# A hybrid DeltaNet and attention block in fp32: VectorE's long elementwise steps made in pieces of at most 256 columns

## The chip, the cores and the metric

The kernel runs on one core of a Trainium2 chip. The metric is the device time of one execution in microseconds (us), lower is better. A core has engines that work side by side: TensorE (PE) for matrix products, with PEld its weight loads; VectorE (DVE), ScalarE (ACT) and GpSimd (POOL) for elementwise work; SyncE (SP), which issues the transfers. They wait for each other by semaphores. Each engine works through its own list of instructions in order.

## The reference

One layer with two groups of heads that read the same normalised input (512 latent tokens and 256 context tokens, 2048 wide) through one projection. Group A, where the change lies, has eight heads of gated DeltaNet: a short convolution over five tokens, silu, gates, and a chunked scan in both directions, added and normalised.

```python
def centred_conv(x, w):                      # five taps, one weight per channel
    pad = CONV_K // 2
    L = x.shape[1]
    xp = jnp.pad(x, ((0, 0), (pad, pad), (0, 0)))
    out = xp[:, 0:L] * w[0]
    for j in range(1, CONV_K):
        out = out + xp[:, j:j + L] * w[j]
    return out
...
    diff = g_c[..., :, None] - g_c[..., None, :]
    decay = jnp.where(incl, jnp.exp(jnp.where(incl, diff, 0.0)), 0.0)
    a = jnp.where(strict, jnp.einsum('nbhid,nbhjd->nbhij', k_beta, k_c) * decay, 0.0)
    t_inv = lax.linalg.triangular_solve(eye + a, ..., lower=True)
...
    def step(s, inp):
        v_new = u_i - jnp.einsum('bhcd,bhde->bhce', w_i, s)
        o_i = (... q_i * exp(g_i) @ s + intra_i @ v_new)
        s = (s * exp(g_last) + (k_i * exp(g_last - g_i))^T @ v_new)
        return s, o_i
...
    o_gdn = (o_lf + flip(o_lb)).astype(h.dtype)
    gdn_lat = (rms_norm(o_gdn, gdn_norm_w).reshape(B, L, GDN_WIDTH) * jax.nn.silu(z_g))
```

Group B is grouped-query attention with eight query heads; both go through one output projection, a gated residual and a last norm.

## The kernel before

**Stages.** Up to about 165 us the norms, the modulation and the first projection; 165 to 290 the first head's convolutions, the gates and its preparation; 290 to 805 the DeltaNet heads, each some 85 us; 805 to 940 the last scan and the preparation of attention; to 1240 attention; to 1412 the output projection.

**Products in three parts.** A fp32 weight piece of 128 x 512 is split into a high part (whi, cast on ScalarE, L122) and a low part (wlo, the difference, L123, made on VectorE for the first 14 pieces and on GpSimd after them); each product is three matmuls. A projection makes the columns of one head, for example k: kl is the latent half (512 columns, L157), kx the context half (256, L159), in 16 steps out of four weight pieces, so wlo_k1_3 is the last low piece for the k of the second head (heads count from 0).

**Convolution** (`conv`, L178). ScalarE copies the projection into craw (L184 the context, L187 the latent part) and makes the first tap for all columns (L195, cacc). VectorE adds taps 1 to 4, in place in cacc (L199): four steps over the 512 latent columns, and for k and v four more over the 256 of the context. ScalarE takes the tanh (L202, L203), VectorE finishes the silu (L212), which gives kq (k and q side by side), kc (k of the context) or vv.

**Preparation of a head** (`gdn_prep`). GpSimd subtracts the gate sums (L550), VectorE takes the minimum with two masks (L553), each over 6 chunks of 64 columns, ScalarE the exponential (L555); VectorE multiplies by a column for each row (L571, 768 columns) and by the products of k and q; then 32 x 32 transposes NT (L587), a series of small steps on NE (L607 to L609) and products for a triangular inverse, with transfers through DRAM in between (nd, NE, DD), ending in DTh (L632), pxah (L640) and UU. The first head's transposes t1h (L509) turn kq; tvh turns vv.

**Scan** (`gdn_scan`). Twelve steps a head. TensorE makes ksh from the state sth, VectorE the right side rh (L731), TensorE tsh (L740), ScalarE vsh (L744), TensorE tsh again (L751), VectorE the next state sth (L757; L755 for the first step). After the last step GpSimd and VectorE (L768) add the two directions, ScalarE takes four sums of squares (L770) and VectorE, GpSimd and ScalarE scale by the norm (L771, L209, L774).

**Order.** TensorE's order is written out: the scan of one head runs between projection matmuls for the next ones, so many columns of them at each yield. The other engines' instructions are put in order by a scheduler that works through what is ready by priority; scan steps on VectorE and ScalarE have high priority (`first_of_all`), the NE series a lower one, and the rest stands in program order of priority. In the attention stage all engines' order is written out. Buffers: cacc and craw rotate, ScalarE's and VectorE's conv steps thus wait for earlier readers.

Of the kernel before, what the change touches and what calls it, by code (L numbers as in the profile page):

```python
# [11 lines left out]
ALU = mybir.AluOpType  # L12
# [10 lines left out]
SEQ = 512  # L23
CTX = 256
# [44 lines left out]
def build(tc, a):  # L69
    nc = tc.nc  # L70
    V, S, G, T, SY = nc.vector, nc.scalar, nc.gpsimd, nc.tensor, nc.sync
# [27 lines left out]
    masks = (cmain[:, 256:320], cmain[:, 320:384])  # L99
# [78 lines left out]
    def conv(t, nm, pl, pc):  # L178

        n = SEQ + (CTX + 2 if pc is not None else 0)  # L180
        off = n - SEQ
        raw = next_craw()
        if pc is not None:
            S.copy(raw[:, 2:2 + CTX], pc)  # L184
        else:
            raw = raw[:, CTX + 2:]
        S.copy(raw[:, off + 2:off + 2 + SEQ], pl)  # L187
        acc = cvp.tile([128, 770], F32, tag="cacc", bufs=CA_BUFS, name=f"cacc_{nm}")
        acc = acc[:, :n]

        def w(j):
            return cvT[:, j * 24 + t:j * 24 + t + 1]

        e = raw[:, 2:]
        S.activation(acc, raw[:, 0:n], AF.Copy, scale=w(0))  # L195
        for i0, m in ((off, SEQ), (0, CTX))[:1 if pc is None else 2]:
            for j in range(1, 5):
                x = acc[:, i0:i0 + m]
                V.scalar_tensor_tensor(out=x, in0=raw[:, i0 + j:i0 + j + m], scalar=w(j), in1=x,  # L199
                                       op0=ALU.mult, op1=ALU.add)  # L200
        if pc is not None:
            S.activation(e[:, :CTX], acc[:, :CTX], AF.Tanh)  # L202
        S.activation(e[:, off:off + SEQ], acc[:, off:], AF.Tanh)  # L203
        return acc, e, off
# [9 lines left out]
    def mul(eng, out, x, y):  # L214
        eng.tensor_tensor(out=out, in0=x, in1=y, op=ALU.mult)  # L215
# [274 lines left out]
    def gdn_prep(h):  # L490
# [6 lines left out]
        gr = gp.tile([128, 12, 64], F32, tag="gr", bufs=1, name=f"gr{nm}")  # L497
# [27 lines left out]
        for p in range(2):  # L525
# [16 lines left out]
        cc = gp.tile([128, 3, 12], F32, tag="cc", bufs=2, name=f"cc{nm}")  # L542
        V.tensor_tensor(out=cc[:, 0].rearrange("p (v q) -> p v q", v=2),
                        in0=gsc["beta"][:, col].rearrange("p (v q) -> p v q", v=2),
                        in1=rk2.unsqueeze(1).to_broadcast([128, 2, 6]), op=ALU.mult)
# [3 lines left out]

        G.tensor_tensor(out=gr, in0=gr, in1=gsc["gcum"][:, col].unsqueeze(2).to_broadcast([128, 12, 64]),  # L550
                        op=ALU.subtract)
        for v in range(2):
            V.tensor_tensor(out=gr[:, v * 6:v * 6 + 6], in0=gr[:, v * 6:v * 6 + 6],  # L553
                            in1=masks[v].unsqueeze(1).to_broadcast([128, 6, 64]), op=ALU.min)
        S.activation(gr, gr, AF.Exp)  # L555

        yield
# [10 lines left out]
            for v in range(2):  # L568
                mul(V, IBv[pr, v, :, 64 - 64 * s:128 - 64 * s], gq[pr, :, 1], grv[pr, v, 2:6])
        AT = gr  # L570
        V.tensor_tensor(out=gr, in0=gr, in1=cc[:, 1].unsqueeze(2).to_broadcast([128, 12, 64]), op=ALU.mult)  # L571
        for v in range(2):
            mul(V, grv[:, v, 2:6], gq[:, :, 0], grv[:, v, 2:6])
        yield
# [28 lines left out]
        with tc.high_priority(offset=1500):  # L603
            for m in range(14, 0, -1):
# [3 lines left out]
                                in1=NE[:, m:m + 1, m + 1:].to_broadcast([96, m, n]), op=ALU.mult)  # L608
# [65 lines left out]
        for p in range(6):  # L674
            for half in range(2):
                b = half * 64
                for v in range(2):
                    i0, o0 = (b + 32, b) if v == half else (b, b + 32)
# [3 lines left out]
        for v in range(2):  # L682
            for half in range(2):
                b = half * 64
                i0, o0 = (b + 32, b) if v == half else (b, b + 32)
# [3 lines left out]
    def gdn_scan(h):  # L689
# [3 lines left out]
        ktok, vtok, cc, sq = pres[h]  # L693
        UU, IB = UUs[h % 2], IBs[h % 2]
        st = None
        o = None
        oq = gp2.tile([128, 2, 4, 128], F32, tag="oq", bufs=1, name=f"oq{nm}")
        osb = oq[:, 0]
        kss = stile([128, 2, 256], f"ks{nm}", "k")
        steps = [(0, 0), (0, 1), (1, 1), (1, 0)] + [(0, p) for p in range(2, 6)] + [(1, p) for p in range(5, 1, -1)]  # L700
        for si, (v, p) in enumerate(steps):
# [6 lines left out]
            if lat and o is None:  # L708
                o = stile([128, 4, 128], f"o{nm}", "o")
            if si == 0:  # L710
                r = vtok[:, p]
            else:
# [11 lines left out]
                with first_of_all():  # L724
# [5 lines left out]
                    for rows, d in halves:  # L730
                        V.scalar_tensor_tensor(out=r[rows], in0=ks[rows, d], scalar=gsc["negeg"][rows, gcol:gcol + 1],  # L731
                                               in1=vtok[rows, p], op0=ALU.mult, op1=ALU.add)
# [32 lines left out]
        oc = gp2.tile([128, 8, 64], F32, tag="oc", bufs=1, name=f"oc{nm}")  # L765
        jk = oc[:, 0:2].rearrange("p c t -> p (c t)")
        G.tensor_tensor(out=oq[:, 1], in0=osb, in1=oq[:, 1], op=ALU.add)
        V.tensor_tensor(out=osb, in0=oq[:, 1], in1=o, op=ALU.add)  # L768
        for p in range(4):
            S.activation(jk, osb[:, p], AF.Square, accum_out=ms[:, p:p + 1])  # L770
        V.scalar_tensor_tensor(out=ms, in0=ms, scalar=1.0 / 128.0, in1=sq, op0=ALU.mult, op1=ALU.add)  # L771
# [641 lines left out]
```

## Time and profile before

| | |
|---|---|
| median of 3 runs | 1405.37 us (1404.99 to 1408.5) |
| the profiled execution | 1413.92 us, its span 1412.1 us |
| TensorE matmuls, weight loads | 1282.5 and 1031.0 us busy, 9406 each |
| VectorE | 747.5 us busy, 1643 instructions |
| ScalarE | 608.3 us busy, 1509 instructions |
| GpSimd | 529.4 us busy, 477 instructions |
| mean granted clock of TensorE | 0.975 |

The page gives busy time by engine and slice; the trace answers which instruction ran when, how long, and what an engine waited for. A row of a timeline is one instruction, or several alike that follow each other; the bracket at its end tells how long the engine had been idle before, and who released it. PE stands for TensorE's matmuls. An instruction's duration includes work that overlaps the next one on its engine, so two starts in a row can be closer than the first one's duration.

### The profile page before, as it was taken

To read this page: it belongs to the slowest core of one execution; us is meant where nothing else is said; L and a number is where in the kernel's file an instruction comes from. 1 tells how busy PE (TensorE), PEld (TensorE's weight loads), DVE (VectorE), ACT (ScalarE), POOL (GpSimd) and SP (SyncE) were. 2 spreads that over 40 slices of the span, in tenths; PEclk is the share of its full clock that TensorE was granted. 3 is DMA by queue.
4 is the path that set the end of the run, shared out by engine and by line. 5 is a ranking of instruction groups with operands and counts; after the bars stand their busy time and mean duration, and the time that the engine had idled before them with its cause. 6 is when DMAs were issued, how large, how long until landed. Compare 5 with 4: busy or idle time off the path is not lost.

```text
span 1412.1 us, 24988 instructions
## 1 busy us (share of the span) xinstructions
PE 1282.5 (91%) x9406; PEld 1031.0 (73%) x9406; DVE 747.5 (53%) x1643; ACT 608.3 (43%) x1509; POOL 529.4 (37%) x477
## 2 busy tenths in 40 slices
PE   3788988999999999999999999889889999999997
PEld 1455676877788787787777877667777778787785
DVE  3434685475456656476665524427566655544322
ACT  4111342445444453544545444446556663433221
POOL 1011211334353453443434445435777772012330
PEclk9999998999999999999999999999999999999999
DMA  9999622222322223232232343353545432474202
GB/s 311 255 270 285 180 72 56 71 56 63 67 71 69 66 65 77 58 84 57 81 66 58 84 127 111 93 186 105 145 132 151 134 97 61 164 234 146 90 33 102
DMA packets 264187, 163.52 MB, mean 116 GB/s; under 512 B 63042, under 2 KB 236187, under 8 KB 263043
## 3 DMA queue, kind: packets, MB, share of 16 engines
q1 hardware_dynamic: 264067, 161.93, 41.6%
q8 instruction: 74, 1.21, 0.4%
q14 instruction: 46, 0.38, 0.1%
HBM read 148.33 MB, written 13.56 MB: 115 GB/s over the span
## 4 chain that ended last, share of the span: by engine, by line
PE 55%; DVE 17%; DMA 8%; issue 8%; ACT 7%; POOL 4%; SPq 2%; POOLq 0%; ACTq 0%; DVEq 0%
PE zl L1197 6%; PE vl L157 5%; DMA wada<-in_w_ada 4%; PE kl L157 3%; PE vx L159 3%; DVE cacc_k L199 2%; DVE cacc_v L199 2%; PE kvl L157 2%; PE po L140 2%; PE tsh L751 2%; PE po L141 2%; PE po L139 2%; PE ql L157 2%; PE kx L159 2%; PE tsh L740 2%
## 5 line engine op out<-in xcount | busy, mean ns | idle before, releaser
L215 POOL TENSOR_TENSOR sdh<-sth,egl 128x256 f32<-128x256 f32 x80 | 55.4, 692 | 169.5 <-DVE sth L757 75.8
L1238 POOL TENSOR_TENSOR gacc<-graw,gacc 128x512 f32<-128x512 f32 x60 | 89.3, 1488 | 43.3 <-ACT graw L1236 30.0
L736 ACT ACTIVATE oqh<-ksh,egsw 64x128 f32<-64x128 f32 x128 | 46.3, 362 | 99.0 <-DVE rh L731 98.2
L731 DVE SCALAR_TENSOR_TENSOR rh<-ksh,negeg,vtokh 64x128 f32<-64x128 f32 x176 | 61.1, 347 | 50.8 <-PE ksh L719 47.5
L1197 PE MATMUL zl<-hhL,whi_z 128*128 128x512 f32 x208 | 88.0, 423 | 0.0
L123 POOL TENSOR_TENSOR wlo_z<-wraw_z,whi_z 128x512 fp32r<-128x512 f32 x52 | 70.5, 1358 | 45.0 <-ACT whi_z L122 43.8
L1197 PE MATMUL zl<-hlL,whi_z 128*128 128x512 f32 x208 | 84.9, 408 | 0.0
L1197 PE MATMUL zl<-hhL,wlo_z 128*128 128x512 f32 x208 | 84.8, 408 | 0.1
L140 PE MATMUL po<-wlo_wo,mh 128*128 128x512 f32 x192 | 77.5, 404 | 3.7 <-DVE wlo_wo L123 3.7
L757 DVE TENSOR_TENSOR sth<-sdh,tsh 128x256 f32<-128x256 f32 x80 | 33.7, 421 | 87.1 <-PE tsh L751 81.7
L139 PE MATMUL po<-whi_wo,mh 128*128 128x512 f32 x192 | 76.0, 398 | 1.5 <-ACT whi_wo L122 1.5
L141 PE MATMUL po<-whi_wo,ml 128*128 128x512 f32 x192 | 76.8, 400 | 0.0
L123 DVE TENSOR_TENSOR wlo_wo<-wraw_wo,whi_wo 128x512 fp32r<-128x512 f32 x48 | 37.7, 794 | 66.5 <-ACT whi_wo L122 66.4
L816 DVE TENSOR_TENSOR ptl<-pt,pth 128x512 fp32r<-128x512 f32 x48 | 31.7, 687 | 72.5 <-ACT pth L815 72.4
L1344 POOL TENSOR_TENSOR yx<-yx,tt 128x512 f32<-128x512 f32 x12 | 17.1, 1443 | 126.9 <-DVE tt L215 67.6
L199 DVE SCALAR_TENSOR_TENSOR cacc_v<-craw,cvT,cacc_v 128x512 f32<-128x512 f32 (+1 forms) x64 | 44.0, 734 | 38.8 <-ACT cacc_v L195 38.5
L751 PE MATMUL tsh<-vsh,ktok 128*128 128x128 f32 x352 | 55.6, 281 | 3.6 <-ACT vsh L744 3.2
L323 POOL TENSOR_TENSOR wlo<-wraw,whi 128x384 fp32r<-128x384 f32 x16 | 16.0, 1006 | 110.4 <-ACT whi L322 110.4
L122 ACT CAST whi_wo<-wraw_wo 128x512 fp32r<-128x512 f32 x48 | 29.3, 618 | 61.4 <-PE po L141 37.7
L751 PEld LDWEIGHTS tsh<-vsh,ktok 128*128 128x128 f32 x352 | 47.8, 192 | 10.1 <-ACT vsh L744 4.6
L255 PE MATMUL ada<-wada,cs 128*32 128x256 f32 x512 | 42.3, 417 | 13.9 <-DMA wada<-in_w_ada 13.8
L744 ACT ACTIVATE vsh<-tsh,cch 128x128 f32<-128x128 f32 x88 | 32.2, 366 | 45.9 <-PE tsh L740 44.9
(488 smaller groups left out, 4162.2 us busy)
## 6 DMA issues: line engine op xcount, KB each, us to landing
wada<-in_w_ada SPq DMA_DIRECT2D x128, 256.0 KB, 5.1
graw<-in_w_ada SPq DMA_DIRECT2D x64, 256.0 KB, 2.7
wraw_z<-in_w_in SPq DMA_DIRECT2D x52, 256.0 KB, 3.1
wraw_wo<-in_w_out SPq DMA_DIRECT2D x48, 256.0 KB, 3.1
wraw_q<-in_w_in SPq DMA_DIRECT2D x28, 256.0 KB, 3.2
wraw_k<-in_w_in SPq DMA_DIRECT2D x28, 256.0 KB, 2.8
wraw_v<-in_w_in SPq DMA_DIRECT2D x28, 256.0 KB, 2.8
xs<-in_x SPq DMA_DIRECT2D x4, 1024.0 KB
```

What stands on the lines that cost most here:

```text
L123: (lo_eng or G).tensor_tensor(out=lo, in0=raw, in1=hi, op=ALU.subtract)
L139: T.matmul(out, lhsT=lh, rhs=rh, start=start, stop=False, skip_group_check=True)
L140: T.matmul(out, lhsT=lh, rhs=rl, start=False, stop=False, skip_group_check=True)
L141: T.matmul(out, lhsT=ll, rhs=rh, start=False, stop=stop, skip_group_check=True)
L157: T.matmul(pl, lhsT=lw, rhs=rt[0][:, k], start=st, stop=sp, skip_group_check=True)
L159: T.matmul(pc, lhsT=lw, rhs=rt[1][:, k], start=st, stop=sp, skip_group_check=True)
L199: V.scalar_tensor_tensor(out=x, in0=raw[:, i0 + j:i0 + j + m], scalar=w(j), in1=x, op0=ALU.mult, op1=ALU.add)
L215: eng.tensor_tensor(out=out, in0=x, in1=y, op=ALU.mult)
L731: V.scalar_tensor_tensor(out=r[rows], in0=ks[rows, d], scalar=gsc["negeg"][rows, gcol:gcol + 1], in1=vtok[rows, p], op0=ALU.mult, op1=ALU.add)
L751: T.matmul(ts[:, d], lhsT=ktok[:, p, half], rhs=vs, start=True, stop=True, skip_group_check=True)
L1197: T.matmul(pl, lhsT=lw, rhs=rt[:, k], start=st, stop=sp, skip_group_check=True)
L1238: G.tensor_tensor(out=acc, in0=raw, in1=acc, op=ALU.add)
```

## The change

Four places of VectorE work on fewer columns at a time, each with more instructions for the same result. In the conv the four latent steps are done for each half of the 512 columns (8 instructions in place of 4). The masks go over 3 chunks of 64 at a time (four of 192 columns in place of two of 384). The product over 768 columns goes in four of 192. The sum of the outputs goes in two of 256. In all VectorE has 1789 instructions in its list in place of 1645 (of which the profile records 1643): 128 are taken away and 272 added. TensorE's order stays the same in every instruction; the scheduler sets the others' order anew.

```diff
@@ conv
-        for i0, m in ((off, SEQ), (0, CTX))[:1 if pc is None else 2]:
+        for i0, m in ((off, 256), (off + 256, 256), (0, CTX))[:2 if pc is None else 3]:
             for j in range(1, 5):
                 x = acc[:, i0:i0 + m]
                 V.scalar_tensor_tensor(out=x, in0=raw[:, i0 + j:i0 + j + m], scalar=w(j), in1=x,
@@ gdn_prep
-        for v in range(2):
-            V.tensor_tensor(out=gr[:, v * 6:v * 6 + 6], in0=gr[:, v * 6:v * 6 + 6],
-                            in1=masks[v].unsqueeze(1).to_broadcast([128, 6, 64]), op=ALU.min)
+        for w0 in range(0, 12, 3):
+            V.tensor_tensor(out=gr[:, w0:w0 + 3], in0=gr[:, w0:w0 + 3],
+                            in1=masks[w0 // 6].unsqueeze(1).to_broadcast([128, 3, 64]), op=ALU.min)
         S.activation(gr, gr, AF.Exp)
@@ gdn_prep
-        V.tensor_tensor(out=gr, in0=gr, in1=cc[:, 1].unsqueeze(2).to_broadcast([128, 12, 64]), op=ALU.mult)
+        for w0 in range(0, 12, 3):
+            mul(V, gr[:, w0:w0 + 3], gr[:, w0:w0 + 3], cc[:, 1, w0:w0 + 3].unsqueeze(2).to_broadcast([128, 3, 64]))
@@ gdn_scan
-        V.tensor_tensor(out=osb, in0=oq[:, 1], in1=o, op=ALU.add)
+        for p in range(0, 4, 2):
+            V.tensor_tensor(out=osb[:, p:p + 2], in0=oq[:, 1, p:p + 2], in1=o[:, p:p + 2], op=ALU.add)
         for p in range(4):
             S.activation(jk, osb[:, p], AF.Square, accum_out=ms[:, p:p + 1])
```

Lines behind line 571 move by one, those behind 768 by two.

VectorE, where the k of head 5 is convolved while the scan of head 3 makes its steps 7 and 8 (heads and steps count from 0). Before:

```order
L199 SCALAR_TENSOR_TENSOR cacc_k5_5856<-craw0_1460,cvT_80,cacc_k5_5856 128x512
L757 TENSOR_TENSOR sth3_7_5927<-sdh3_7_5894,tsh3_7_5913 128x256
L199 SCALAR_TENSOR_TENSOR cacc_k5_5856<-craw0_1460,cvT_80,cacc_k5_5856 128x256
L212 SCALAR_TENSOR_TENSOR kq5_5852<-craw0_1460,cacc_k5_5856 128x4x64 x2
L212 SCALAR_TENSOR_TENSOR kc5_5853<-craw0_1460,cacc_k5_5856 128x2x64
L632 STREAM_TRANSPOSE DTh4_5744<-DDh4_5743 128x384
L731 SCALAR_TENSOR_TENSOR rh3_8_5942<-ksh3_5404,negeg_87,vtokh3_4646 64x128 x2
L212 SCALAR_TENSOR_TENSOR kc5_5853<-craw0_1460,cacc_k5_5856 128x2x64
```

And after the change, in the same place:

```order
L199 SCALAR_TENSOR_TENSOR cacc_k5_5944<-craw0_1460,cvT_80,cacc_k5_5944 128x256 x8
L758 TENSOR_TENSOR sth3_7_6019<-sdh3_7_5986,tsh3_7_6005 128x256
L199 SCALAR_TENSOR_TENSOR cacc_k5_5944<-craw0_1460,cvT_80,cacc_k5_5944 128x256
L212 SCALAR_TENSOR_TENSOR kq5_5940<-craw0_1460,cacc_k5_5944 128x4x64
L199 SCALAR_TENSOR_TENSOR cacc_k5_5944<-craw0_1460,cvT_80,cacc_k5_5944 128x256
L212 SCALAR_TENSOR_TENSOR kq5_5940<-craw0_1460,cacc_k5_5944 128x4x64
L732 SCALAR_TENSOR_TENSOR rh3_8_6034<-ksh3_5487,negeg_87,vtokh3_4716 64x128 x2
L633 STREAM_TRANSPOSE DTh4_5832<-DDh4_5831 128x384
L212 SCALAR_TENSOR_TENSOR kc5_5941<-craw0_1460,cacc_k5_5944 128x2x64 x2
```

The scan's rh of step 8 moved ahead of the transpose DTh and of both kc.

ScalarE, at the end of the scan of head 3 and the start of that of head 4, where the v of head 5 is convolved (whi_q1a is a weight piece for attention). Before:

```order
L770 ACTIVATE och3_6317,msh3_6316<-oqh3_5403 128x128 x3
L555 ACTIVATE grh5_6390<-grh5_6390 128x768
L770 ACTIVATE och3_6317,msh3_6316<-oqh3_5403 128x128
L774 ACTIVATE oqh3_5403<-oqh3_5403,msh3_6316 128x128 x4
L187 COPY craw0_1460<-vl5_6009 128x512
L744 ACTIVATE vsh4_0_6383<-tsh4_0_6381,cch4_5512 128x128
L184 COPY craw0_1460<-vx5_6010 128x256
L122 CAST whi_q1a_2_6455<-wraw_q1a_2_6453 128x512
L195 ACTIVATE cacc_v5_6355<-craw0_1460,cvT_80 128x770
```

And after the change:

```order
L772 ACTIVATE och3_6413,msh3_6412<-oqh3_5486 128x128 x4
L555 ACTIVATE grh5_6491<-grh5_6491 128x768
L776 ACTIVATE oqh3_5486<-oqh3_5486,msh3_6412 128x128 x4
L122 CAST whi_q1a_2_6556<-wraw_q1a_2_6554 128x512
L184 COPY craw0_1460<-vx5_6106 128x256
L187 COPY craw0_1460<-vl5_6105 128x512
L745 ACTIVATE vsh4_0_6484<-tsh4_0_6482,cch4_5595 128x128
L195 ACTIVATE cacc_v5_6452<-craw0_1460,cvT_80 128x770
```

All four squares now precede the exponential, and the weight cast and both copies precede vsh.

VectorE, in the first head's preparation (IB, grh and NTh are its tiles, q1 belongs to the second head). Before:

```order
L553 TENSOR_TENSOR grh0_1677<-grh0_1677,cmain_77 128x384 x2
L199 SCALAR_TENSOR_TENSOR cacc_q1_1697<-craw0_1460,cvT_80,cacc_q1_1697 128x512
L532 TENSOR_SCALAR skh0_1762<-ssh0_1680 128x2
L123 TENSOR_TENSOR wlo_k1_3_1908<-wraw_k1_3_1905,whi_k1_3_1907 128x512
L199 SCALAR_TENSOR_TENSOR cacc_q1_1697<-craw0_1460,cvT_80,cacc_q1_1697 128x512
L539 RECIPROCAL rk2h0_1769<-skh0_1762 128x6
```

And after the change, where wlo_k1_3 stands now:

```order
L212 SCALAR_TENSOR_TENSOR kq1_1707<-craw0_1460,cacc_q1_1709 128x4x64 x2
L215 TENSOR_TENSOR IB0_1575<-gqh0_1811,grh0_1689 64x4x64 x2
L215 TENSOR_TENSOR grh0_1689<-grh0_1689,cch0_1789 128x192 x4
L215 TENSOR_TENSOR grh0_1689<-gqh0_1811,grh0_1689 128x256 x2
L215 TENSOR_TENSOR grh0_1689<-gch0_1866,grh0_1689 128x128 x2
L588 STREAM_TRANSPOSE NTh0_1693<-grh0_1689 32x6x32 x4
L123 TENSOR_TENSOR wlo_k1_3_1929<-wraw_k1_3_1926,whi_k1_3_1928 128x512
```

The low weight piece moved from among the q1 conv steps to behind the transposes NTh.

## Rows read from the trace of the kernel before

**Rows 1.** The page, part 1: busy us, share of the span and instructions of each engine.

```profile
PE 1282.5 (91%) x9406; PEld 1031.0 (73%) x9406; DVE 747.5 (53%) x1643; ACT 608.3 (43%) x1509; POOL 529.4 (37%) x477
```

**Rows 2.** The windows by stage, of all engines. Columns: stretch, its length, then busy us and instructions of each engine, the granted clock of TensorE, the share of the DMA engines, GB/s.

```profile
165.00:290.00 125.00, 112.30 (x904) 93.27 (x903) 84.36 (x261) 51.82 (x147) 24.36 (x23) 0.93 0.27 64
...
550.00:635.00 85.00, 80.25 (x744) 66.93 (x743) 52.47 (x128) 40.58 (x114) 35.38 (x34) 1.00 0.28 69
```

**Rows 3.** TensorE's waits between 290 and 940 us: line that waited, whom it waited for, us in total, times, longest.

```profile
PE tsh L740 <- DVE rh L731: 14.3, 16, 2.1
PE ksh L722 <- DVE sth L755: 5.1, 4, 2.3
...
PE kvx L159 <- ACT craw L184: 3.0, 2, 2.6
```

**Rows 4.** The same in the first head's stretch, 165 to 290 us.

```profile
PE gtr L431 <- ACT egl L427: 2.5, 1, 2.5
PE pxah L640 <- DVE DTh L632: 2.2, 1, 2.2
PE gcp L416 <- issue: 1.9, 1, 1.9
```

**Rows 5.** VectorE's groups by line and form: busy us, mean ns of one, idle time before them.

```profile
L199 DVE SCALAR_TENSOR_TENSOR cacc_v<-craw,cvT,cacc_v 128x512 f32<-128x512 f32 x32 | 26.2, 819 | 38.6 <-ACT cacc_v L195 38.5
...
L199 DVE SCALAR_TENSOR_TENSOR cacc_q<-craw,cvT,cacc_q 128x512 f32<-128x512 f32 x32 | 24.1, 752 | 12.7 <-ACT cacc_q L195 12.4
L199 DVE SCALAR_TENSOR_TENSOR cacc_v<-craw,cvT,cacc_v 128x256 f32<-128x256 f32 x32 | 20.7, 648 | 0.2
L199 DVE SCALAR_TENSOR_TENSOR cacc_k<-craw,cvT,cacc_k 128x256 f32<-128x256 f32 x32 | 20.2, 632 | 0.1
```

**Rows 6.** Timeline of VectorE in the first head, the k conv between steps of the gates. Columns: start, duration in us, engine, line, instruction, count.

```profile
170.79 0.48 DVE L199 SCALAR_TENSOR_TENSOR cacc_k<-craw,cvT,cacc_k 128x256 f32<-128x256 f32 x1
171.19 0.22 DVE L400 RECIPROCAL s_g<-s_g 128x12 f32<-128x12 f32 x1
...
172.48 0.75 DVE L199 SCALAR_TENSOR_TENSOR cacc_k<-craw,cvT,cacc_k 128x512 f32<-128x512 f32 x1
173.14 0.17 DVE L403 TENSOR_SCALAR ug<-w_g 128x12 f32<-128x12 f32 x1
```

**Rows 7.** Timeline of VectorE, the q conv of a middle head, and one v conv of the second head.

```profile
237.88 4.33 DVE L199 SCALAR_TENSOR_TENSOR cacc_v<-craw,cvT,cacc_v 128x512 f32<-128x512 f32 x8 [2.00 <-ACT cacc_v L195]
...
573.38 2.33 DVE L199 SCALAR_TENSOR_TENSOR cacc_q<-craw,cvT,cacc_q 128x512 f32<-128x512 f32 x3 [2.96 <-ACT cacc_q L195]
575.74 0.42 DVE L757 TENSOR_TENSOR sth<-sdh,tsh 128x256 f32<-128x256 f32 x1
```

**Rows 8.** Timeline of TensorE, a middle head, where it waits for rh of step 8.

```profile
565.48 0.46 PE L740 MATMUL tsh<-rh,UU 128*128 128x128 f32 x2 [1.40 <-DVE rh L731]
```

**Rows 9.** Timeline of VectorE ahead of that.

```profile
561.77 2.27 DVE L212 SCALAR_TENSOR_TENSOR kq<-craw,cacc_k 128x256 f32<-128x256 f32 x2
563.97 0.28 DVE L212 SCALAR_TENSOR_TENSOR kc<-craw,cacc_k 128x128 f32<-128x128 f32 x1
564.17 0.57 DVE L632 STREAM_TRANSPOSE DTh<-DDh 128x384 f32<-128x384 f32 x1
564.67 0.67 DVE L731 SCALAR_TENSOR_TENSOR rh<-ksh,negeg,vtokh 64x128 f32<-64x128 f32 x2
```

**Rows 10.** Timeline of ScalarE at the change of scans in a middle head.

```profile
592.65 0.85 ACT L555 ACTIVATE grh<-grh 128x768 f32<-128x768 f32 x1 [0.81 <-POOL wlo_q1a L123]
593.40 0.29 ACT L770 ACTIVATE och<-oqh 128x128 f32<-128x128 f32 x1
...
595.11 1.28 ACT L774 ACTIVATE oqh<-oqh,msh 128x128 f32<-128x128 f32 x4 [1.32 <-POOL msh L209]
...
596.76 0.36 ACT L744 ACTIVATE vsh<-tsh,cch 128x128 f32<-128x128 f32 x1
...
597.79 0.95 ACT L195 ACTIVATE cacc_v<-craw,cvT 128x770 f32<-128x770 f32 x1
```

**Rows 11.** Timeline of TensorE there.

```profile
597.17 0.71 PE L751 MATMUL tsh<-vsh,ktok 128*128 128x128 f32 x4 [0.81 <-ACT vsh L744]
...
600.21 0.70 PE L722 MATMUL ksh<-sth,kc 128*128 128x256 f32 x2 [0.93 <-DVE sth L755]
```

**Rows 12.** Timeline of TensorE in head 2, where kvx waits for the copy of v's projection.

```profile
333.94 0.38 PE L159 MATMUL kvx<-hhC,whi_kv 128*128 128x256 f32 x1 [2.62 <-ACT craw L184]
```

**Rows 13.** Timeline of VectorE in the first head: wlo_k1_3, and the transposes NTh.

```profile
197.22 0.67 DVE L123 TENSOR_TENSOR wlo_k<-wraw_k,whi_k 128x512 fp32r<-128x512 f32 x1
...
204.91 1.57 DVE L587 STREAM_TRANSPOSE NTh<-grh 32x192 f32<-32x192 f32 x4
```

**Rows 14.** Timeline of TensorE there: the first matmul on wlo_k1_3, and tvh.

```profile
203.00 0.39 PE L157 MATMUL kl<-hhL,wlo_k 128*128 128x512 f32 x1
...
204.63 0.41 PE L620 MATMUL tvh<-cmain,vv 128*128 128x128 f32 x2 [1.11 <-DVE grh L215]
```

**Rows 15.** Windows in the first head; the granted clock stands behind the engines' columns.

```profile
178.00:182.00 4.00, 3.25 (x15) 3.04 (x16) 2.35 (x9) 0.94 (x6) 0.00 (x0) 0.62 0.47 131
182.00:186.00 4.00, 4.00 (x11) 2.54 (x9) 2.39 (x6) 0.63 (x1) 0.00 (x0) 0.53 0.26 67
236.00:240.00 4.00, 3.69 (x11) 2.46 (x10) 2.12 (x4) 1.80 (x3) 1.27 (x1) 0.50 0.19 43
```

## The prediction

> **What bounds the kernel now.** I read the page's busy shares first: TensorE is busy 91% of the span, VectorE 53% [rows 1]. Then the table by stretches: where a middle head runs, TensorE works 80.25 of 85 us and VectorE 52.47, and the first head's stretch is the loosest with 112.30 of 125 [rows 2]. TensorE's order is written out and the change leaves it as it is. So a longer VectorE costs nothing by itself. It counts only where TensorE stands still for something that VectorE or ScalarE hands over later, or earlier, than before. The list of TensorE's waits names these places: in 290 to 940 us the scan's right side rh (14.3 us in 16 waits), the first state step sth of line 755 (5.1) and the copy craw ahead of kvx (3.0) [rows 3]; in the first head the gate sums gtr, the product pxah and gcp, with 2.5, 2.2 and 1.9 us [rows 4]. The sum is made of these waits.
>
> **What the pieces cost on VectorE.** By their own durations a 512-column conv step takes 752 to 819 ns and a 256-column one 632 to 648 [rows 5], but these durations overlap the next instruction, and some contain a wait for GpSimd. Better is start to start. With an independent instruction behind it, a 256-column step gives way after 171.19 − 170.79 = 0.40 us and a 512-column one after 173.14 − 172.48 = 0.66 [rows 6]. Cutting a 512 thus costs 2 × 0.40 − 0.66 = 0.13 us. But steps that follow each other on the same columns are slower: three 512-column q steps in a chain take 575.74 − 573.38 = 2.36 us, 0.79 each [rows 7]. After the change the halves alternate, so that neighbours are independent and the chain's price falls away.
> - q conv (8 of them): 4 × 0.79 = 3.15 before, 8 × 0.40 = 3.17 after. Nothing.
> - k and v conv (16): four long and four short steps took 4.33 us [rows 7]; twelve short ones take 12 × 0.40 = 4.8, that is +0.5 each and about +8 us in all.
> - masks (L553) 2 to 4 pieces, product (L571) 1 to 4, output sum (L768) 1 to 2: at 0.13 for an added piece 2 × 0.13 + 3 × 0.13 + 0.13 = 0.8 a head at most, 6 in all.
>
> VectorE gets some 11 to 14 us more, and 144 added instructions × 0.13 = 19 is the ceiling. Little of it lies where TensorE waits, and the scheduler has moved scan steps between the pieces, which is worth more.
>
> **Heads 5 to 7, k conv.** TensorE waits 1.40 us at 565.48 for rh_8 [rows 8]. VectorE was late there because kq (2.27 us for two), one kc and the transpose DTh stood in front of rh [rows 9]. In the new order rh_8 stands ahead of DTh and of both kc (first order difference of the change's section). But more conv steps and both kq still stand in front of it. Ahead of rh_8 the conv now takes +0.5; DTh (0.50 start to start) and one kc (0.20) fall away, and a 256-column step in place of a 512 in front of rh_7 starts that side 0.27 earlier, of which little is left at rh_8. I take −0.35 a head, −1.05 for three. Bounds: −1.40 a head if the wait goes altogether, +0.3 if the pieces cost more than they free.
>
> **Heads 5 to 7, output sum and v conv.** The sum in halves lets all four squares (L770) run before the exponential (L555); the fourth ran behind it, at 593.40, and the scaling L774 followed it by way of VectorE and GpSimd at 595.11 [rows 10]. With the square some 1.5 us earlier, L774 is held by the exponential's own end, and starts 0.75 to 0.9 earlier. In the new ScalarE order a weight cast and both copies to craw then precede vsh (second order difference), so vsh stays about at 596.8 and its wait of 0.81 at 597.17 remains [rows 10, 11]. But L195, the conv's first tap, comes 0.7 earlier, and with it line 755, whose wait of 0.93 [rows 11] goes. The twelve pieces return about 0.4 at the next step. Net −0.5 a head, −1.5 for three; bounds −0.93 and +0.5.
>
> **Head 2** has no previous scan in that place: kvx waits 2.62 us for the copy behind L774 [rows 12]. The same 0.9 us goes there, and some of the second wait of line 755 too: −1.25, with −0.35 for its k conv as above, −1.6. **Heads 3 and 4**: a silu half comes newly ahead of a rh, +0.2 each (half a 256-column step), v between +0.1 and −0.2: +0.3. **The last scan** saves 0.2 by its sum in halves.
>
> **First head.** Here the order changes most. The gate chain ran between 512-column steps; behind 256-column ones, with half of the q0 conv put behind it, it ends about 1.1 us earlier, out of the 1.9 us wait of gcp [rows 4]. In exchange, seven of q0's eight pieces stand behind the gates' row copy L433, so that TensorE waits some 3 us at t1h, which it reaches 1.1 us earlier to 1.2 us later than before. And wlo_k1_3, made at 197.22, now stands behind the transposes NTh (204.91, 1.57 us; third order difference), while TensorE wants it at 203.00 [rows 13, 14]. The transposes end at 206.5 − 0.6 (its own place is free), plus 0.67 for itself: TensorE goes on at 206.5, and reaches tvh 0.35 later, at 206.85 in place of 204.63: +2.2. Behind that, pxah waits for the DMA chain of the triangular inverse, with 2.2 us of room for TensorE [rows 4], so most is given back: +0.5 to +1.9. With 0.1 at the next product I take +1.5; bounds −4 and +8, from the rivals.
>
> The clock is in that bound. [...]
>
> **Sum**: −1.05 − 1.5 − 1.6 + 0.3 − 0.2 + 1.5 = −2.55 us. The profiled execution took 1413.92 us with a span of 1412.1, and would come to 1411.4; the median of the runs shown is 1405.37, 0.6% less. The same waits in it give 1402.8, and I say 1403.
>
> [...] The rows show that a second piece costs 0.13 us at independent neighbours [rows 6]. [...]
>
> **Rivals.**
> - *Nearly nothing, as summed* (0.55): 1403; its own range is 1400 to 1408, since waits move by tenths.
> - *Faster: the gate chain closes the gcp wait, and the clock stays up* (0.22). For: the wait is only 1.9 us, and 1.1 goes. Against: TensorE waits at t1h soon after. It gives 3.1 back and takes the first head's +1.5 to −1: 1402.8 − 3.1 − 2.5 = 1397. If rh_8's wait goes whole, as much as 3 × 1.05 comes on top: 1394.
> - *Slower: the first head starves* (0.19). Mechanism: wlo_k1_3 and t1h late by 3.5 and 3 us, each followed by a stretch at half clock (3.1), and pxah's chain late too, so that nothing is given back. It decides from the point where the NE series, not TensorE, still ends last: if the series slips with TensorE, 1405.4 − 4.05 (the sum without the first head) + 2.2 + 1.2 + 2 × 3.1 = 1411.
> - *Slower: each piece pays in full* (0.04): were VectorE last everywhere, the 19 us of 144 × 0.13 come to the end, 1424. Against: VectorE is idle for 32 of 85 us in a head [rows 2], and q costs nothing even on the path. [...]
> - That the pieces merge again is out: the order holds every piece.
>
> **How the numbers follow.** About 0.3%, 4.2 us, is what a measurement here can tell from no change. Below 1401.2 lie most of the second case (0.19) and a tail of the first (0.08): faster 0.27. Above 1409.6 lie 0.15 of the third, the fourth with 0.04, and 0.02 of the first: slower 0.21. Same 0.52. The range 1396.5 to 1412 leaves out half of the second case (0.1), the third's upper end (0.05) and the fourth.
>
> **What would show it.** In the changed profile the wait of TensorE for rh_8 in the heads from 550 us on should be about 1.05, not 1.40 and not 0; the waits for line 755 gone from three heads; kvx's wait under 2 us; in the first head waits of some 3 us at t1h and at a kl product for wlo_k. VectorE's busy time should grow by a dozen us, but TensorE's stretches from 550 to 805 shrink by less than 1 us each. I am wrong if a middle head's 85 us grows (pieces on the path), if the first head's 125 us moves by more than 4 (clock), or if the attention from 940 on, which the change doesn't touch, moves by more than 1.

## The result, and the profile after

The changed kernel takes 1417.22 us in the median of its runs, the kernel before 1409.83 beside it: a ratio of 1.0042 with a 95% interval of 1.0028 to 1.0057. The ratio is not that of the two medians (1.0052); it is estimated over all runs but one of the changed kernel that took 1570 us at a granted clock of 0.754. That is slower by some 5.9 us (0.0042 x 1410), just past the bound of 0.3%; the forecast was 1403 and no difference. The two profiled executions hide it: their spans are 1412.6 (after) and 1412.1 us (before), because the stage up to 165 us, which the change doesn't touch, came out 4 us shorter in the later one, and what follows the last of the four rows below 1.7 us shorter. TensorE's order is the same in both, so the loss is found by the start of the same matmul. These rows are the first of gtp, the first of pxah, one of head 5's kl and one of kvl, before:

```profile
166.08 0.30 PE L374 MATMUL gtp<-cmain,gso 32*128 32x32 f32 x2
...
233.75 0.26 PE L640 MATMUL pxah<-DTh,grh 32*32 32x32 f32 x2 [2.24 <-DVE DTh L632]
...
550.02 0.39 PE L157 MATMUL kl<-hhL,whi_k 128*128 128x512 f32 x1
...
804.98 0.39 PE L157 MATMUL kvl<-hhL,whi_kv 128*128 128x512 f32 x1
```

and after:

```profile
162.11 0.28 PE L374 MATMUL gtp<-cmain,gso 32*128 32x32 f32 x2 [0.33 <-DVE gso L372]
...
233.39 0.25 PE L641 MATMUL pxah<-DTh,grh 32*32 32x32 f32 x1 [2.43 <-DVE DTh L633]
...
552.29 0.39 PE L157 MATMUL kl<-hhL,whi_k 128*128 128x512 f32 x1
...
807.16 0.39 PE L157 MATMUL kvl<-hhL,whi_kv 128*128 128x512 f32 x1
```

From gtp to pxah, the first head, the kernel before takes 233.75 − 166.08 = 67.67 us and the changed one 71.28: +3.6. In that stretch TensorE is busy for 58.47 us before and 58.39 after, at a mean granted clock of 0.92 in both, and idle for 9.20 and 12.89: the 3.6 us are waiting. From pxah to kl it is 316.27 and 318.90: +2.6. The three middle heads behind that take 254.96 and 254.87, no difference. The length of the first head in one execution is worth no better than 3 us, its idle time is steadier (see the table below).

TensorE's waits in the first head after the change, to be set beside [rows 4]:

```profile
PE t1h L509 <- DVE kq L212: 3.3, 1, 3.3
PE kl L157 <- DVE wlo_k L123: 3.1, 1, 3.1
PE pxah L641 <- DVE DTh L633: 2.4, 1, 2.4
PE gtr L431 <- ACT egl L427: 1.7, 1, 1.7
...
PE gcp L416 <- PE ql L157: 0.5, 1, 0.5
```

and from 290 to 940 us, beside [rows 3]:

```profile
PE tsh L741 <- DVE rh L732: 12.6, 18, 2.1
PE ksh L723 <- DVE sth L758: 6.3, 4, 1.6
...
PE ksh L723 <- DVE sth L756: 2.3, 1, 2.3
PE kvx L159 <- ACT craw L184: 1.9, 2, 1.5
```

Two waits of over 3 us are new in the first head, at t1h and at a kl product that wants a wlo_k; gcp's fell from 1.9 to 0.5 and gtr's from 2.5 to 1.7. Behind it, the first state step (now line 756) fell from 5.1 to 2.3 us as forecast, kvx from 3.0 to 1.9 and rh from 14.3 to 12.6; but the later state steps (line 758) now make TensorE wait 6.3 us ahead of ksh, up to 1.6 at a time.

VectorE's busy time rose from 747.5 us [rows 1] to 773.7, 26 for 144 instructions; part of it is longer instructions beside one of GpSimd, as below (1.84 us in place of 0.75 at one place).

```profile
PE 1278.5 (91%) x9406; PEld 1026.6 (73%) x9406; DVE 773.7 (55%) x1787; ACT 611.5 (43%) x1509; POOL 519.2 (37%) x477
```

**First head.** VectorE makes wlo_k1_3 only behind the transposes, as the order said:

```profile
200.70 1.57 DVE L588 STREAM_TRANSPOSE NTh<-grh 32x192 f32<-32x192 f32 x4
202.30 0.69 DVE L123 TENSOR_TENSOR wlo_k<-wraw_k,whi_k 128x512 fp32r<-128x512 f32 x1
```

and TensorE stands in front of it (kl), then goes on to tvh without the wait that it had in [rows 14]:

```profile
203.04 0.80 PE L157 MATMUL kl<-hhL,wlo_k 128*128 128x512 f32 x1 [3.12 <-DVE wlo_k L123]
...
203.85 0.63 PE L621 MATMUL tvh<-cmain,vv 128*128 128x128 f32 x2
```

What followed was not the resynchronisation that was forecast. VectorE's rows before, of k1's conv and the first and last step of the NE series:

```profile
210.27 4.33 DVE L199 SCALAR_TENSOR_TENSOR cacc_k<-craw,cvT,cacc_k 128x512 f32<-128x512 f32 x8 [0.32 <-ACT cacc_k L195]
...
216.04 0.16 DVE L607 TENSOR_TENSOR tmh<-NEh 96x14 f32<-96x14 f32 x1
...
225.04 0.17 DVE L609 TENSOR_TENSOR NEh<-NEh,tmh 96x14 f32<-96x14 f32 x1
```

and after:

```profile
211.54 3.26 DVE L199 SCALAR_TENSOR_TENSOR cacc_k<-craw,cvT,cacc_k 128x256 f32<-128x256 f32 x8 [5.52 <-ACT cacc_k L195]
214.71 0.17 DVE L608 TENSOR_TENSOR tmh<-NEh 96x14 f32<-96x14 f32 x1
...
225.18 0.17 DVE L610 TENSOR_TENSOR NEh<-NEh,tmh 96x14 f32<-96x14 f32 x1
```

From gtp the series began 216.04 − 166.08 = 49.96 us later before and 214.71 − 162.11 = 52.60 after, and ended at 58.96 and 63.07. It stands behind the conv of k1 on VectorE, that conv behind the copy of kl, and kl behind the missing weight piece. Of the 4.1 us at its end 2.6 were there at its start; the rest came inside the series, where four conv steps and both kq now stand between its steps. So pxah's chain slipped by as much as TensorE, and pxah still waits 2.4 us. The granted clock was low behind both new waits, 0.59 for 181 to 185 us after t1h and 0.50 for 203 to 207 after kl, as it was before after gcp, with 0.62 and 0.53 for 178 to 186 [rows 15]:

```profile
177.00:181.00 4.00, 1.16 (x5) 0.58 (x4) 3.94 (x12) 0.63 (x1) 0.00 (x0) 1.00 0.33 80
181.00:185.00 4.00, 3.55 (x13) 3.07 (x14) 3.86 (x12) 3.17 (x10) 1.30 (x1) 0.59 0.32 90
203.00:207.00 4.00, 3.96 (x13) 3.47 (x14) 2.85 (x10) 0.62 (x2) 0.00 (x0) 0.50 0.44 92
```

Behind the wait for gtr it goes the other way: for 214 to 222 us the clock was 0.81 and 0.76 before, and is 1.00 after the change.

**Later heads.** TensorE waits for rh of step 8 a third of a microsecond less than in [rows 8]:

```profile
567.64 0.46 PE L741 MATMUL tsh<-rh,UU 128*128 128x128 f32 x2 [1.07 <-DVE rh L732]
```

TensorE at the change of scans, beside [rows 11]: the wait for line 756 at 601.18 is gone, and eight microseconds later stands a new one of 1.60.

```profile
599.11 0.71 PE L752 MATMUL tsh<-vsh,ktok 128*128 128x128 f32 x4 [0.46 <-ACT vsh L745]
...
601.18 0.70 PE L723 MATMUL ksh<-sth,kc 128*128 128x256 f32 x2
...
609.25 0.70 PE L723 MATMUL ksh<-sth,kc 128*128 128x256 f32 x2 [1.60 <-DVE sth L758]
```

VectorE ahead of it:

```profile
605.99 1.00 DVE L199 SCALAR_TENSOR_TENSOR cacc_v<-craw,cvT,cacc_v 128x256 f32<-128x256 f32 x2
606.91 1.84 DVE L212 SCALAR_TENSOR_TENSOR vv<-craw,cacc_v 128x256 f32<-128x256 f32 x2
608.78 0.42 DVE L758 TENSOR_TENSOR sth<-sdh,tsh 128x256 f32<-128x256 f32 x1
```

The two silus vv take 1.84 us where they took 0.75 in the kernel before, and sth is queued behind them. VectorE and GpSimd at this place before:

```profile
605.42 0.75 DVE L212 SCALAR_TENSOR_TENSOR vv<-craw,cacc_v 128x256 f32<-128x256 f32 x2
606.20 0.42 DVE L757 TENSOR_TENSOR sth<-sdh,tsh 128x256 f32<-128x256 f32 x1
...
606.70 0.61 POOL L215 TENSOR_TENSOR sdh<-sth,egl 128x256 f32<-128x256 f32 x1 [3.98 <-PE t3h L522]
607.28 1.34 POOL L123 TENSOR_TENSOR wlo_k<-wraw_k,whi_k 128x512 fp32r<-128x512 f32 x1
```

GpSimd and ScalarE after the change, at the same time as vv:

```profile
606.86 1.28 POOL L123 TENSOR_TENSOR wlo_k<-wraw_k,whi_k 128x512 fp32r<-128x512 f32 x1 [3.03 <-ACT whi_k L122]
609.28 0.62 POOL L215 TENSOR_TENSOR sdh<-sth,egl 128x256 f32<-128x256 f32 x1 [1.15 <-DVE sth L758]
```

```profile
605.33 0.63 ACT L203 ACTIVATE craw<-cacc_v 128x512 f32<-128x512 f32 x1
...
606.12 0.61 ACT L122 CAST whi_k<-wraw_k 128x512 fp32r<-128x512 f32 x1
607.02 0.42 ACT L202 ACTIVATE craw<-cacc_v 128x256 f32<-128x256 f32 x1 [0.30 <-DVE cacc_v L199]
```

GpSimd's subtraction wlo_k of the next weight piece begins at 606.86, 0.05 us ahead of vv, and in front of sdh; its cast (L122, 606.12) went ahead of the context's tanh (L202, 607.02) on ScalarE, in the new order. The order of the kernel before has sdh first on GpSimd and the cast (606.11) behind L202 (605.53) on ScalarE.

### The profile page after: what moved, and what is told of

It reads as the page before. It is cut to its first block, busy times and chain, and to the rows that moved or that the text cites. A ratio compares the mean times of both kernels' runs of the same rounds, so it can differ in the third digit from the quotient of the medians.

```text
span 1412.6 us, 25146 instructions
## 1 busy us (share of the span) xinstructions
PE 1278.5 (91%) x9406; PEld 1026.6 (73%) x9406; DVE 773.7 (55%) x1787; ACT 611.5 (43%) x1509; POOL 519.2 (37%) x477
## 4 chain that ended last, share of the span: by engine, by line
PE 33%; DVE 13%; issue 7%; ACT 5%; DMA 4%; POOL 4%; SPq 0%; POOLq 0%; ACTq 0%; DVEq 0%
PE zl L1199 5%; PE vl L157 3%; PE po L140 2%; PE po L141 2%; PE po L139 2%; DMA graw<-in_w_ada 2%; DVE cacc_v L199 2%; POOL gacc L1240 1%; DVE cacc_k L199 1%; PE vx L159 1%; PE kl L157 1%; PE tsh L752 1%; DVE rh L732 1%; DVE tmh L608 1%; PE tsh L741 1%
## 5 line engine op out<-in xcount | busy, mean ns | idle before, releaser
L215 POOL TENSOR_TENSOR sdh<-sth,egl 128x256 f32<-128x256 f32 x80 | 52.3, 654 | 174.2 <-DVE sth L758 117.6
L818 DVE TENSOR_TENSOR ptl<-pt,pth 128x512 fp32r<-128x512 f32 x48 | 31.7, 688 | 69.8 <-ACT pth L817 69.7
L199 DVE SCALAR_TENSOR_TENSOR cacc_v<-craw,cvT,cacc_v 128x256 f32<-128x256 f32 x96 | 47.9, 547 | 39.6 <-ACT cacc_v L195 39.1
L199 DVE SCALAR_TENSOR_TENSOR cacc_k<-craw,cvT,cacc_k 128x256 f32<-128x256 f32 x96 | 53.8, 603 | 10.5 <-ACT cacc_k L195 10.0
L122 ACT CAST whi_wo<-wraw_wo 128x512 fp32r<-128x512 f32 x48 | 29.3, 618 | 61.7 <-PE po L141 39.5
## 6 DMA issues: line engine op xcount, KB each, us to landing
wada<-in_w_ada SPq DMA_DIRECT2D x128, 256.0 KB, 5.3
graw<-in_w_ada SPq DMA_DIRECT2D x64, 256.0 KB, 2.6
wraw_z<-in_w_in SPq DMA_DIRECT2D x52, 256.0 KB, 3.1
wraw_wo<-in_w_out SPq DMA_DIRECT2D x48, 256.0 KB, 2.7
wraw_q<-in_w_in SPq DMA_DIRECT2D x28, 256.0 KB, 3.1
wraw_k<-in_w_in SPq DMA_DIRECT2D x28, 256.0 KB, 2.8
wraw_v<-in_w_in SPq DMA_DIRECT2D x28, 256.0 KB, 2.8
```

## The experiments

The theory from these rows (**places**): two places lose, the first head by its new order, and the state step behind vv in each later head by the collision with GpSimd; the pieces as such cost TensorE next to nothing, and the output sum in halves gains. The rival (**pieces**): every added instruction costs alike. All ratios are to the kernel before, on the same chip.

**e1_conv** splits the conv alone:

```diff
--- before
-        for i0, m in ((off, SEQ), (0, CTX))[:1 if pc is None else 2]:
+        for i0, m in ((off, 256), (off + 256, 256), (0, CTX))[:2 if pc is None else 3]:
```

> Conv steps in halves alone; masks, product and output sum whole as before. Places theory (two places lose: the first head's new order costs 3.6 us, the v steps of heads 2 to 6 cost 3.3 us between them): wlo_k1_3 stands ahead of the q1 conv here, so TensorE's wait of 3.1 us for wlo_k goes, that of 3.3 us at t1h stays, and the first head costs about 1 us; without the sum in halves v starts no earlier, so the gains of 1 us at line 755 and of 1.1 us at kvx are gone while the later sth still comes 1 us or more late in each head: +5 to +8 us, ratio 1.004 to 1.006. Pieces theory (each added instruction pays alike): 96 of 144 instructions, 2/3 of 5.9 us, +3.9 us, 1.0028.

Measured 1.0056 (1.0036 to 1.0076), in the range of the places theory and above the figure of the other. The waits that the sum in halves had removed (line 755, kvx) are back, and a new one at line 757 is there. It is not the one that was forecast: only one of its four, in head 4, is 1.4 us behind a vv of 1.84; the three in the later heads are 0.7 each, with no collision ahead of sth:

```profile
PE ksh L722 <- DVE sth L755: 4.3, 4, 2.3
PE ksh L722 <- DVE sth L757: 3.5, 4, 1.4
...
PE kvx L159 <- ACT craw L184: 3.0, 2, 2.6
```

**e2_rest** is the other half: masks, product and sum in pieces, and the conv line of the kernel before.

```diff
--- after
-        for i0, m in ((off, 256), (off + 256, 256), (0, CTX))[:2 if pc is None else 3]:
+        for i0, m in ((off, SEQ), (0, CTX))[:1 if pc is None else 2]:
```

> Masks, product and output sum in pieces, conv whole. Places theory: the first head keeps its old order and the wait for wlo_k and t1h stays small; kvx in head 2 and line 755 in the later heads wait 1 us less, and the eight conv steps of v end early enough: -1 to -5 us, ratio 0.9965 to 0.9993. Pieces theory: 48 of 144 instructions, +2.0 us, 1.0014.

Measured 0.9981 (0.9965 to 0.9997): faster, with 48 instructions added. That rules out that every added instruction costs alike.

**e3_late** keeps the whole change, except that the convs of the first two heads are whole:

```diff
--- after
-        for i0, m in ((off, 256), (off + 256, 256), (0, CTX))[:2 if pc is None else 3]:
+        parts = ((off, 256), (off + 256, 256)) if int(nm[1:]) >= 2 else ((off, SEQ),)
+        for i0, m in parts if pc is None else parts + ((0, CTX),):
```

> The whole change, but the convs of the first two heads in whole 512 steps. Places theory: the first head falls back to its old waits, 3.6 us come off and the later heads' +2.3 remain, ratio about 1.0016 with the stretch of 165 to 290 us as before. Pieces theory: 24 of 144 instructions fewer, +4.9 us, 1.0035.

Measured 1.0021 (1.0004 to 1.0037): by the middle of the intervals about half of the loss comes with the convs of the first two heads. TensorE's wait at t1h is 0.88 us here, and none is left for wlo_k.

**e4_lo** leaves all pieces and moves two weight pieces:

```diff
--- after
-        (lo_eng or G).tensor_tensor(out=lo, in0=raw, in1=hi, op=ALU.subtract)
+        with tc.high_priority(offset=400 if nm in ('k1_2', 'k1_3') else 0):
+            (lo_eng or G).tensor_tensor(out=lo, in0=raw, in1=hi, op=ALU.subtract)
```

> The whole change, and the low weight pieces wlo_k1_2 and wlo_k1_3 with a higher priority, which puts both ahead of the q1 conv in VectorE's order. Places theory: TensorE's wait of 3.1 us for wlo_k falls under 0.5, the chain behind it (conv of k1, NE series, DTh, pxah) comes earlier by 2 to 3 us, so +3 to +4 us in all, ratio 1.002 to 1.003. Pieces theory: as many instructions, 1.0042 stays. If the pxah chain doesn't hang on that wait, the time stays too, with the wait of 2.4 at pxah grown.

Measured 1.0024 (1.001 to 1.0039). wlo_k1_3 is made at 189.54, no kl product waits, the wait at t1h is as before, and pxah's chain came earlier with TensorE rather than leave it a longer wait:

```profile
PE t1h L510 <- DVE kq L213: 3.3, 1, 3.3
...
PE pxah L642 <- DVE DTh L634: 2.2, 1, 2.2
```

**e5_lo_dve** takes GpSimd's colliding subtraction to VectorE, all else of the change kept:

```diff
--- after
+        if nm[0] == 'k' and nm.endswith('_0') and nm[1] in '34567':
+            lo_eng = V
         (lo_eng or G).tensor_tensor(out=lo, in0=raw, in1=hi, op=ALU.subtract)
```

> The whole change, and of each later head (3 to 7) the first low weight piece of k is subtracted on VectorE and no longer on GpSimd; it stands there behind the silu vv, and nothing else moves. Collision theory (vv, two inputs from SBUF, stands still while GpSimd's subtraction runs, and the state step sth behind it with TensorE): vv x2 falls from 1.84 us to about 0.75, TensorE's wait of 1.6 us for the second sth of a head falls to about 0.5, 1 us less in each of four heads, -3.5 to -4 us against the whole change: ratio 1.0015 to 1.002. Conv theory (the twelve v steps themselves are late): the wait of 1.6 stays, ratio 1.004.

Measured 1.0021 (1.0003 to 1.0039). VectorE has one 512-column instruction more in each such head, and TensorE waits less. VectorE and TensorE at the same place as above:

```profile
602.64 0.75 DVE L214 SCALAR_TENSOR_TENSOR vv<-craw,cacc_v 128x256 f32<-128x256 f32 x2
603.43 0.42 DVE L760 TENSOR_TENSOR sth<-sdh,tsh 128x256 f32<-128x256 f32 x1
...
604.61 0.68 DVE L125 TENSOR_TENSOR wlo_k<-wraw_k,whi_k 128x512 fp32r<-128x512 f32 x1
```

```profile
603.90 0.70 PE L725 MATMUL ksh<-sth,kc 128*128 128x256 f32 x2 [0.53 <-DVE sth L760]
```

vv is back at 0.75 us and the wait fell from 1.60 to 0.53. The collision is 1.1 us of it, the twelve steps are the rest. The same execution holds a place that was not repaired: at 770.66 GpSimd subtracts a piece for attention (wlo_kv), two vv beginning at 770.70 take 1.84 us again, and TensorE waits 1.63 for sth. GpSimd's order alone doesn't make it: e7_sum (below) has wlo_k ahead of sdh too, but there the first two vv, the last at 599.25, are done before wlo_k begins at 600.00. Counted from the kl of the four rows above, vv begins at 55.4 us before, at 53.4 in e7_sum and at 54.6 after the change; the subtraction begins at 57.3, 54.9 and 54.6, and in e1_conv still at 57.2. So in heads 5 to 7 it takes both: the sum in halves, behind which the subtraction comes 2.4 us earlier, and the twelve v steps, which put vv 1.2 later again.

**e9_both** puts both repairs into the whole change (the two edits above in one).

> The whole change with all its pieces, and both repairs together: wlo_k1_2 and wlo_k1_3 with a higher priority, and the first low weight piece of k in heads 3 to 7 on VectorE. Places theory: the repairs took 2.5 us (1.0024) and 3 us (1.0021) off the 5.9; they lie in different stretches and add: +0 to +1 us, ratio 0.9995 to 1.001. If both act on the same slack, or the pieces cost something of their own: 1.002 as with either.

Measured 1.0002 (0.9987 to 1.0018): with every piece kept, the loss against the kernel before is gone. Either repair alone leaves an interval that overlaps that of the whole change; both together are clear of it. The pieces are not free for all that. This kernel also holds the sum in halves, which alone stands at 0.9969 (e7_sum, below), and the two intervals don't touch: the other 136 instructions, with both repairs, still cost some 0.3%. A part of it is seen: TensorE's idle time in the first head is 11.1 us against 8.9 in e7_sum, and the collision with wlo_kv, which the edit doesn't move, costs a wait of 1.61 us. No run divides the rest between the order and a price of the pieces themselves.

**e7_sum** and **e10_sum4** look for the gain: the kernel before with the output sum in halves (the line of the diff above), or in four.

```diff
--- before
-        V.tensor_tensor(out=osb, in0=oq[:, 1], in1=o, op=ALU.add)
+        for p in range(4):
+            V.tensor_tensor(out=osb[:, p], in0=oq[:, 1, p], in1=o[:, p], op=ALU.add)
```

> The output sum in halves alone, all else as before; ScalarE's order is that of the whole change at the squares and copies. Places theory: the whole gain of the masks-and-sum version, -2 to -4 us, ratio 0.997 to 0.9985, with kvx waiting 1.1 us less and line 755 no longer waited for in the later heads. If the masks made the gain: 1.000.

> Only the output sum in four parts of 128 columns, one for each square. ScalarE's order is that of the sum in halves. Order theory (the gain is that the fourth square precedes the exponential): the same as in halves, ratio 0.9965 to 0.9975. Pipe theory (the gain is that the first square starts on a shorter sum): 0.2 to 0.3 us more in each of seven heads, 0.9955.

The halves measured 0.9969 (0.9956 to 0.9983), 8 instructions that make the fastest of all kernels that were run; the quarters 0.9984 (0.9968 to 0.9999). The intervals overlap: four parts bring nothing beyond two, which speaks for the order and against the pipe. ScalarE in the version with halves, to be set beside [rows 10]: the fourth square precedes the exponential, L775 begins 1.12 us behind the exponential's start where L774 began 2.46 behind it, and L195 follows 2.7 us behind it as before (597.79 − 595.11).

```profile
586.75 0.31 ACT L771 ACTIVATE och<-oqh 128x128 f32<-128x128 f32 x1
...
587.79 0.85 ACT L555 ACTIVATE grh<-grh 128x768 f32<-128x768 f32 x1 [0.63 <-POOL wlo_q1a L123]
588.91 1.28 ACT L775 ACTIVATE oqh<-oqh,msh 128x128 f32<-128x128 f32 x4 [0.27 <-POOL msh L209]
...
591.61 0.93 ACT L195 ACTIVATE cacc_v<-craw,cvT 128x770 f32<-128x770 f32 x1
```

**e8_masks** has masks and product in pieces alone.

```diff
--- after
-        for i0, m in ((off, 256), (off + 256, 256), (0, CTX))[:2 if pc is None else 3]:
+        for i0, m in ((off, SEQ), (0, CTX))[:1 if pc is None else 2]:
...
-        for p in range(0, 4, 2):
-            V.tensor_tensor(out=osb[:, p:p + 2], in0=oq[:, 1, p:p + 2], in1=o[:, p:p + 2], op=ALU.add)
+        V.tensor_tensor(out=osb, in0=oq[:, 1], in1=o, op=ALU.add)
```

> Masks and product in pieces alone, all else as before; the orders of ScalarE and GpSimd are those of before at the squares, copies and weight pieces. Places theory: nothing that TensorE waits for moves, 0.9995 to 1.0005. Pieces theory: 40 added instructions, +1.6 us, 1.0012.

Measured 1.0012 (0.9994 to 1.0029), which can't be told from none, nor from the 1.0012 of the pieces theory: this run decides nothing between them. In the profile the three middle heads took 1.1 us more; four masks take 0.14 us longer ahead of the exponential (2.25 for 2.11), and TensorE's wait for vsh behind it grows by as much (0.94 for 0.81 in each head).

**e6_kq_late** was meant as the best version: the parts of e2_rest, and the halves for q and k of heads 2 to 7.

```diff
--- after
-        for i0, m in ((off, 256), (off + 256, 256), (0, CTX))[:2 if pc is None else 3]:
+        parts = ((off, 256), (off + 256, 256)) if nm[0] != "v" and int(nm[1:]) >= 2 else ((off, SEQ),)
+        for i0, m in parts if pc is None else parts + ((0, CTX),):
```

> Masks, product and output sum in pieces; conv in halves for q and k of heads 2 to 7 alone, v and the first two heads whole. Places theory: the gain of the masks-and-sum version (-2.7 us) plus 0.3 to 0.4 us for the earlier rh of step 8 in each of five or six heads: -4 to -5 us, ratio 0.9965 to 0.997. Pieces theory: 96 instructions added, +3.9 us, 1.0028. If the k steps bring nothing by themselves: 0.998.

Measured 1.0000 (0.9985 to 1.0015), a miss: the halves of k and q bring nothing and lose what e2_rest gained in heads 2 to 4. From head 5 on its profile has 0.33 us less at rh of step 8 and 0.15 more at the state step ahead of it; in heads 3 and 4 the state steps take 0.57 and 0.44 more, and rh of step 8 gains nothing. That is not all of the 2.5 us by which pxah to kl is longer than in e2_rest; the rest was not found in the waits.

The lengths of the stretches, each worked out as above from the same four matmuls, in one execution of each kernel, and TensorE's idle time in the first of them:

| | gtp to pxah | of it idle | pxah to kl | kl to kvl | ratio |
|---|---|---|---|---|---|
| before | 67.7 | 9.2 | 316.3 | 255.0 | 1 |
| after | 71.3 | 12.9 | 318.9 | 254.9 | 1.0042 |
| e1_conv | 67.8 | 10.7 | 318.8 | 258.4 | 1.0056 |
| e2_rest | 65.7 | 10.3 | 314.9 | 252.6 | 0.9981 |
| e3_late | 65.5 | 10.0 | 319.6 | 254.8 | 1.0021 |
| e4_lo | 66.4 | 11.1 | 318.6 | 254.9 | 1.0024 |
| e5_lo_dve | 69.8 | 12.6 | 317.0 | 253.0 | 1.0021 |
| e6_kq_late | 66.1 | 9.4 | 317.4 | 252.7 | 1.0000 |
| e7_sum | 65.9 | 8.9 | 315.0 | 251.6 | 0.9969 |
| e8_masks | 65.1 | 9.6 | 316.7 | 256.0 | 1.0012 |
| e9_both | 69.3 | 11.1 | 317.7 | 253.0 | 1.0002 |
| e10_sum4 | 65.1 | 9.7 | 315.4 | 251.8 | 0.9984 |

Seven kernels have the first head's old conv: 65.1 to 67.7 us long, idle for 8.9 to 10.3, mean 9.6. The two with the late weight piece are idle for 12.9 and 12.6, the three with the new conv order but an early weight piece for 10.7, 11.1 and 11.1. So the late weight piece is some 1.8 us of waiting and the rest of the new order, t1h's wait above all, 1.3. The lengths vary more, by the clock: e4_lo and e9_both have all but the same order and the same idle time there, but are 66.4 and 69.3 us long, with TensorE busy for 55.4 us at a mean granted clock of 0.97 and for 58.2 at 0.93.

## Why the prediction was wrong

The rule that TensorE's waits decide and not VectorE's busy time held: +26 us on VectorE came to +5.9. The steps that failed are two: the return behind v's twelve pieces, put at 0.4 us a head, and the first head's +1.5, of which pxah was to give most back. Step by step:

- *VectorE some 11 to 14 us more, ceiling 19*: mis-sized. It was 26.2, or 0.18 us for each of 144 instructions and not 0.13: 18.8 in e1_conv where 8 were forecast, 9.7 in e8_masks where some 5 were, 1.2 in e7_sum as forecast. At undisturbed places the 0.40 of a step holds (eight in 3.26 us at 211.54). Little of it lay where TensorE waits.
- *k conv, −0.35 a head*: right. The wait at 565.48 [rows 8] was 1.40 and is 1.07 at 567.64; the state step ahead of it waits 0.14 more, so some −0.2 net.
- *output sum and v's start*: right in its mechanism. The wait of 0.93 [rows 11] went, that of vsh fell from 0.81 to 0.46, and kvx's wait from 2.62 [rows 12] to 1.54. e7_sum shows the sum in halves alone as a gain of 0.31%.
- *"The twelve pieces return about 0.4 at the next step"*: this step failed. The wait there is 1.60: 0.5 by the pieces themselves, near the forecast, and 1.1 because GpSimd's weight subtraction now runs beside vv (e5_lo_dve). The prediction walked VectorE's and ScalarE's order of that place; GpSimd's, where the same piece had moved ahead of sdh, is not in it. So heads 5 to 7 gained nothing in place of 2.55, as the row of kl to kvl says.
- *Heads 3 and 4, +0.3, and head 2, −1.6*: mis-sized. From pxah to kl it is +2.6 in place of −1.3. The kvx gain came, but was returned at the waits for vsh of step 1 (0.8 each in heads 2 and 3), behind the tanh of v that stands ahead of it on ScalarE, at the state steps, and by the collision in head 4 (1.43). Over that stretch TensorE's waits grew by 1.5 us in all; the other 1.1 were not traced.
- *First head, +1.5, since "most is given back" at pxah*: this step failed too, and the third rival's condition held instead: the NE series slipped with TensorE. t1h's wait (3.3, forecast some 3) and the wait for wlo_k (3.1, forecast 3.5) came as worked out; counted from gtp, t1h began 0.8 us earlier, within its bounds. What was wrong was to read pxah's 2.2 us as room. The wait showed only that DTh came last, not that its chain was free of what TensorE was late with; e4_lo shows the dependence: without the wait for wlo_k the chain came earlier, and pxah waits 2.2 us as before. The third rival's price was not borne out: 9.6 us for the first head, of which 3.6 came. That its 1411 lies 5.6 us above the 1405.4 that it starts from, near the measured 5.9, is luck: it kept −4.05 for the later heads, which came to +2.5.
- *The clock*, for which the sum has no term: it came out even in these two executions. The stretch at a low clock at 178 us (0.62 and 0.53) went and one behind t1h came (0.59); the wait for wlo_k added another at 203 us (0.50), and the one at 214 us (0.81 and 0.76) went. Busy time is 58.47 and 58.39 us. No run shows the 3.1 us that two rivals' sums take for such a stretch: 0.62 and 0.53 for 4 us each [rows 15] are some 3.4 us lost (an estimate, 4 x 0.38 + 4 x 0.47).
- *What would show it*: apart from VectorE's dozen all the signs that were named came, the waits at rh_8, line 755, kvx, t1h and wlo_k among them, and the time was wrong all the same: they stand at places that were on the list, and what the sum had missed stood at line 757 (758 after the change) and in pxah's chain. Of the signs of being wrong, the attention's 1 us was passed (1.4 us shorter from its first pt matmul to the end, 468.3 and 466.9), but that can't be laid to the change: with the attention untouched too it is 466.6 in e7_sum and 472.9 in e3_late.
- *The rival in which each piece pays in full*: a price of each piece is not what decided. e2_rest and e7_sum have more instructions and are faster (0.9981 and 0.9969), and e9_both has every one of the 144 and no loss (1.0002). Such a price can have a part in the 0.3% between e9_both and e7_sum, which no run divides.

## What to carry to other kernels

Cutting long instructions of an engine that is off the critical path was cheap here beside what it did to the order: every queue has to be read again behind it, the one that nothing was changed on too, and most of all where two engines' instructions can stand in each other's way. A wait in front of a product is room only if the chain that it waits for doesn't begin behind the thing that is late. And the parts of a change should be timed apart: here one of four, 8 instructions of 144, held all the gain that was found. A change that comes out even can hide a gain and a loss: with both repairs the whole was at 1.0002, and the gain in it at 0.9969.

## What the runs showed of the hardware

Two silus on VectorE with both inputs in SBUF took 1.84 us where a GpSimd subtraction of 1.28 us began within 0.05 us of them, and 0.75 without it (the kernel before, and e5_lo_dve). What held them up was not shown. The length of the first head varied by 2.9 us between two executions with all but the same order and the same idle time there (e4_lo and e9_both): TensorE's granted clock behind the wait of 2.2 us at gtr was 0.63 for 214 to 218 us in e9_both and 1.00 in e4_lo. So the length of this stretch is not one number, and its idle time, 11.1 us in both, is the steadier measure.
